# Two VectorE steps in other places: the residues of the first FFN weight pair cut in two, the sums of the second pair behind two residues of h

## The chip, the cores and the metric

One Trainium2 chip, of which the kernel uses one core. The metric is the device time of one execution in microseconds. The kernel before takes 1040.91 us, the median of 3 runs (1039.49 to 1041.45). The profile is of one further execution, which took 1038.12 us.

## The reference

One layer of a streaming encoder, in float32, for 256 rows of 2048. The input is normalised and multiplied by w_in (2048 x 5120). One part of the result goes through differential attention with 4 heads, the other through a gated causal convolution. Both results stand side by side in `mixed`, and then:

```python
h = h + jnp.einsum('bsm,md->bsd', mixed, w_out[l])
hn = rms_norm(h, norm2_g[l])
a = jnp.einsum('bsd,df->bsf', hn, w_gate[l])
bu = jnp.einsum('bsd,df->bsf', hn, w_up[l])
h = h + jnp.einsum('bsf,fd->bsd', jax.nn.silu(a) * bu, w_down[l])
```

w_out is 2048 x 2048, w_gate and w_up are 2048 x 5632, w_down is 5632 x 2048. Each weight is used once, for all 256 rows.

## The kernel before

**How a product is made.** Each float32 operand is split into a rounded part and a residue: `hi = round(a)` in a type that TensorE multiplies fast, and `lo = a - hi`. A product is then three matmuls into one PSUM bank: hi x hi, lo x hi and hi x lo. For weights, a chunk of 128 x 1024 (512 KB) is loaded by SyncE into `raw`. ScalarE casts it to `whi` (L351), and VectorE subtracts to get `wlo` (L360). For some chunks, marked `by_dma`, the residue is made without VectorE: ScalarE writes the negative rounded part (L354), and POOL issues a DMA that adds the weights to it out of memory (L355).

**Pairs and twos.** The FFN's products are run in blocks of 512 columns, each block for w_gate and w_up together (or for two column blocks of w_down). In a block, some of the rows of the weights are multiplied by a scheme of Strassen's kind with seven products instead of eight. Such a unit is a *pair* (letter s in the order of units): SyncE loads 1 MB into `wb` (four slices of 512 columns). VectorE forms the sums of slices (`pair_sums`, L1054 to L1056), three new ones in `wt` and one that replaces the first slice of `wb`. ScalarE rounds: three slices of `wb` in L1063, the replaced one in L1067, the three of `wt` in L1068, together `wh`. VectorE makes the residues `wl` in two instructions, four slices in L1072 and three in L1073. TensorE then runs seven products of three matmuls each (L1090, L1091, L1092). The remaining rows of the weights are plain units, *twos* (g for w_gate, u for w_up; a capital letter means that the residue is made by DMA): twelve matmuls each, L1114 with `whi` and L1119 with `wlo`. The first block's order is s g G u s g s G U s U u.

**The seam.** The last 512 columns of w_out are a block of eight chunks of twelve matmuls each (L390 and L391 with `whi`, L396 with `wlo`). Behind it the first FFN block begins with a pair. Around this seam:

- `make_forms` prepares the left operands of the pairs (`fhi`, `flo`) out of `hn`, the first half of the scaled rows of h, and at its end the sums, casts and residues of the first pair.
- `out_done(3)` runs when the last w_out columns stand in PSUM: VectorE adds them to h (L883), ScalarE scales the result (L894), TensorE transposes four blocks of it (L902) into a PSUM bank `ps_h`, twice. For each of the two banks ScalarE writes the rounded part (L910, two instructions), and VectorE the residue (L912, two instructions, `llo`). Later the squares of h are summed (ScalarE L528, VectorE L926), POOL turns them into the norm `rest` (L226, L227, L928), and only then does POOL issue its next residue DMA (L355).
- A bank of PSUM is reused in turn. The pair's seventh product takes the bank of the first `ps_h`, so it waits for the first two L912. A later u unit takes the bank of the second `ps_h`.

**What sets the order.** Every engine runs its list in the order in which the program emits it, waiting at each instruction for semaphores. The emission is done by `run_chunks`: before each unit `t` is multiplied, it emits the loads, sums, casts and residues of units up to some number ahead (`until(...)`), and at points inside `multiply` it calls `resume()`, which lets each running generator (`make_forms`, `out_done`, ...) go on to its next `yield`. `lag(n)` is n such yields. So a VectorE instruction's place depends on which yield emits it. `part_of(i)` emits the residues of unit i, `round_of(i)` its casts, `sums_of(i)` the sums of a pair. `raw` has four buffers in turn in the FFN, and `wb` two; a load waits until the last reader of its buffer is done, and the loads wait in one queue, SyncE's.

Of the kernel before, what the change touches and what calls it, by code (L numbers as in the profile page):

```python
# [19 lines left out]
P = 128  # L20
# [97 lines left out]
def tile_block(  # L118
# [331 lines left out]
    def sums_of(i):  # L450
        c = chunks[i]
        if "sides" in c and "t" not in c:
            load_until(i + 1, True)
            o = earlier(pair_at, i, 1)
            if o is not None:
                part_of(o)
            pair_sums(c)
# [12 lines left out]
    def round_of(i):  # L470
        if i not in rounded:
            rounded.add(i)
            load_until(i + 1, True)
            sums_of(i)
            chunks[i]["round"](chunks[i])

    def part_of(i):
        if i not in parted:
            parted.add(i)
            round_of(i)  # L480
            chunks[i]["split"](chunks[i])

    def run_chunks():
        n = len(chunks)
        pair_at.extend(i for i, c in enumerate(chunks) if "sides" in c)
        two_at.extend(i for i, c in enumerate(chunks) if "kind" in c and "sides" not in c)
        at = dict(part=0, dma=0, sums=0, round=0, minus=0, raw=0)
        first = next(i for i, c in enumerate(chunks) if "kind" in c)

        def until(what, do, stop, only=lambda c: True, may=lambda i: True):  # L490
            while at[what] < min(n, stop) and may(at[what]):
                if only(chunks[at[what]]):
                    do(at[what])
                at[what] += 1

        for t in range(n):
            if t >= first - AHEAD:
                until("part", part_of, t + 1 + (LO_AHEAD if t >= first else 1))
                until("raw", lambda i: round_raw(chunks[i]), t + 1 + RAW_AHEAD, lambda c: "sides" in c,
                      lambda i: i <= t or may_round_raw(t, i))  # L500
                ahead = SUMS_AHEAD if t >= first else 0
                until("sums", sums_of, t + 1 + ahead - ("sides" in chunks[t] and bool(chunks[t].get("prompt"))), may=may_sum)
                until("dma", round_of, t + 1 + DMA_AHEAD, lambda c: c["by_dma"])
                until("round", round_of, t + 1 + (HI_AHEAD if t > first else LO_AHEAD))
                load_until(t + 1 + LOAD_AHEAD)
            else:
                if t < len(XPARTS):
                    until("part", part_of, t + 2)
                else:
                    until("part", part_of, t + 1 + AHEAD)  # L510
                    until("minus", minus_of, min(t + 1 + MINUS_AHEAD, first), lambda c: c.get("minus"))
                    until("round", round_of, min(t + 1 + ROUND_AHEAD, first))
            part_of(t)
            chunks[t]["multiply"](chunks[t])
            if chunks[t].get("prompt") and chunks[t]["done"]:
                resume()
        while running:
            resume()
# [359 lines left out]
    def out_done(n, ps):  # L878
        cs = slice(n * N, (n + 1) * N)
        if n == D // N - 1:  # L880
            open_second()
        for m in range(NM):
            dve.tensor_tensor(h[m][:, cs], h[m][:, cs], ps[m], ALU.add)  # L883
        for m in range(NM):
            pool.dma_start(out=out[m * P : (m + 1) * P, cs], in_=h[m][:, cs])
        if n == 2:
            held[0] -= NM
        if n == 0:
            yield from open_first()
        elif n < D // N - 1:  # L890
            yield
        scaled = ffn["scaled"]
        for m in range(NM):
            act.activation(scaled[:, m], h[m][:, cs], AF.Copy, scale=rstd1[m])  # L894
        yield from lag(2)
        for t in range(0, N // P, 2):
            k = n * (N // P) + t
            yield from room(1)
            pt = aux_ps.tile([P, 2, S], F32, tag="aux", name="ps_h")
            for i in range(2):  # L900
                for m in range(NM):
                    pe.transpose(pt[:, i, m * P : (m + 1) * P], scaled[:, m, (t + i) * P : (t + i + 1) * P], ident)  # L902
            if n % 2 == 0:
                rows = ffn["hn"][:, n // 2 * NS + t : n // 2 * NS + t + 2, :]
                for i in range(2):
                    act.activation(rows[:, i, :], pt[:, i, :], AF.Copy, scale=col("g2", k + i))
            else:
                hi, lo = (a[:, t : t + 2] for a in ffn["plain"][0]) if n == 1 else lhs_two("h", k)
                for i in range(2):
                    act.activation(hi[:, i], pt[:, i], AF.Copy, scale=col("g2", k + i))  # L910
                for i in range(2):
                    dve.scalar_tensor_tensor(lo[:, i], pt[:, i], col("g2", k + i), hi[:, i].bitcast(F32),  # L912
                                             ALU.mult, ALU.subtract)
                    hT[k + i] = (hi[:, i, :], lo[:, i, :])
            yield
        if n == 2:
            start(make_forms())
        if n == D // N - 1:
            yield from lag(2)
        for m in range(NM):  # L920
            square_sum(h[m][:, cs], ss2[m][:, n : n + 1])
        if n == D // N - 1:
            yield
            for m in range(NM):
                ss = small.tile([P, 1], F32, tag="ssh", name="ssh")
                dve.tensor_reduce(ss, ss2[m], AX.X, ALU.add)  # L926
                rsqrt_mean(rest[m], ss, D, EPS)
                pool.tensor_tensor(rest[m], rest[m], rms1[:, m : m + 1], ALU.mult)  # L928
            open_third()
            yield from lag(10)  # L930
            at = slot[0] % (KD // 2) * 4 - 2 * 4
            for a, c in zip(arena, ffn["plain"][1]):
                act.copy(c, a[:, at : at + 8].rearrange("p (k m) c -> p k (m c)", m=NM))
            for k in REST:
                i, k_ = divmod(k, HK)
                plain[k] = tuple(c[:, k_ - NS] for c in ffn["plain"][i])
# [75 lines left out]
    def make_forms():  # L1012
# [25 lines left out]
        sums_of(pair_at[0])  # L1038
        round_raw(first)
        yield  # L1040
        part_of(pair_at[0])

    def load_pair(c):
# [21 lines left out]
    def round_pair(c):  # L1065
        round_raw(c)
        act.copy(c["hi"][:, 3], c["b"][:, 0])  # L1067
        act.copy(c["hi"][:, :3], c["t"])  # L1068

    def split_pair(c):  # L1070
        c["lo"] = ffn["w", c["turn"]].tile([P, 7, N], F32R, tag="wl", name="wl")
        dve.tensor_tensor(c["lo"][:, 3:], c["b"], c["hi"][:, 3:].bitcast(F32), ALU.subtract)  # L1072
        dve.tensor_tensor(c["lo"][:, :3], c["t"], c["hi"][:, :3].bitcast(F32), ALU.subtract)  # L1073

    def sum_bank(c, i):
        sums = c["sums"]
# [268 lines left out]
```

## Time and profile before

| what | before |
|---|---|
| median of the runs | 1040.91 us (1039.49 to 1041.45) |
| profiled execution | 1038.12 us |
| its span | 1036.3 us |
| TensorE busy | 1024.2 us, 99% |
| VectorE busy | 890.0 us, 86% |
| ScalarE busy | 707.9 us, 68% |
| POOL busy | 166.8 us, 16% |
| moved by DMA | 260.68 MB, 252 GB/s in the mean |

All times in the profile's rows are microseconds from the start of the span. In a timeline row the columns are start, duration, engine, line, operation, output<-inputs, shape, count, and in brackets the engine's idle time before the row with what ended it. A row of waits reads: who waited <- for whom: microseconds in total, times, the longest. A row of a window gives the window, its length, and the busy time and the number of instructions of TensorE, its weight loads, VectorE, ScalarE and POOL. Behind them stand the granted TensorE clock (1.00 is full speed), the DMA engines' busy share and GB/s. A row of DMA issues gives destination<-source, the queue, the count, KB each, and the microseconds from issue to landing. Ends of matmuls are modelled and overlap, so the distance between starts is what is counted.

### The profile page before, as it was taken

The page shows a single profiled execution, that of the slowest core. Times are in us where ns is not written, and L with a number is a line of the kernel's source. Part 1 is how long each engine was busy: PE and PEld are TensorE (multiplying, and loading weights), DVE is VectorE, ACT ScalarE, POOL GpSimd, SP SyncE. Part 2 cuts the span into 40 slices and gives each one's busy share as a digit, 9 for nine tenths or more (in the row PEclk, how much of TensorE's full clock was granted, in tenths as well). Part 3 has the DMA queues.
Part 4 walks back from the last instruction along what each step waited for, and adds up shares of the span by engine and source line. Part 5 has one row for each costly group of instructions (what it writes and reads, how often), then busy time and mean ns, then how long its engine had stood idle before and what let it go on. Part 6 is the DMA issues. An engine that isn't in the chain of part 4 may idle for free. (4 is left out here: it accounts for less than half of the span.)

```text
span 1036.3 us, 13143 instructions
## 1 busy us (share of the span) xinstructions
PE 1024.2 (99%) x4621; PEld 845.8 (82%) x4621; DVE 890.0 (86%) x1120; ACT 707.9 (68%) x940; POOL 166.8 (16%) x206
## 2 busy tenths in 40 slices
PE   9999999999999899999999999999999999999998
PEld 7888887888887688888888888888888888888887
DVE  6699889897648888999989889999898887998984
ACT  7754567857758667777665757776766576767761
POOL 0150332411100221011002020110110221101122
PEclk9999999999999999999999999999999999999999
DMA  9968665675565898798799997987979999789896
GB/s 364 311 203 247 225 204 183 193 213 183 162 228 179 291 315 241 245 311 234 251 284 253 304 265 268 312 238 247 305 236 282 271 266 329 221 266 302 236 263 131
DMA packets 65490, 260.68 MB, mean 252 GB/s; under 512 B 7312, under 2 KB 8592, under 8 KB 56976
## 3 DMA queue, kind: packets, MB, share of 16 engines
q1 hardware_dynamic: 47648, 202.13, 53.2%
q0 software_dynamic: 17344, 57.16, 29.7%
q8 instruction: 36, 0.59, 0.2%
q10 hardware_dynamic: 432, 0.55, 0.1%
q14 instruction: 30, 0.25, 0.1%
HBM read 251.42 MB, written 8.39 MB: 251 GB/s over the span
## 5 line engine op out<-in xcount | busy, mean ns | idle before, releaser
L351 ACT CAST whi<-raw 128x1024 fp32r<-128x1024 f32 (+1 forms) x246 | 253.9, 1040 | 46.3 <-PE acc L391 25.9
L360 DVE TENSOR_TENSOR wlo<-raw,whi 128x1024 fp32r<-128x1024 f32 (+1 forms) x153 | 184.0, 1208 | 45.6 <-ACT whi L351 39.8
L1063 ACT CAST wh<-wb 128x1536 fp32r<-128x1536 f32 x66 | 97.9, 1484 | 127.8 <-issue 66.3
L1072 DVE TENSOR_TENSOR wl<-wb,wh 128x2048 fp32r<-128x2048 f32 x66 | 151.0, 2287 | 37.9 <-ACT wh L1067 37.5
L355 POOL DMA_DIRECT2D wlo<-in_wts_dram x79 | 69.8, 883 | 541.9 <-ACT wlo L354 397.3
L390 PE MATMUL acc<-whi,lhi 128*128 128x512 f32 x352 | 139.0, 395 | 0.3 <-ACT whi L351 0.3
L391 PE MATMUL acc<-whi,llo 128*128 128x512 f32 x352 | 137.3, 390 | 0.0
L1090 PE MATMUL q<-wh,fhi 128*128 128x512 f32 x308 | 120.2, 390 | 2.4 <-DVE llo L912 2.4
L1092 PE MATMUL q<-wl,fhi 128*128 128x512 f32 x308 | 119.9, 389 | 0.0
L1091 PE MATMUL q<-wh,flo 128*128 128x512 f32 x308 | 119.8, 389 | 0.0
L1073 DVE TENSOR_TENSOR wl<-wt,wh 128x1536 fp32r<-128x1536 f32 x66 | 115.6, 1752 | 0.0
L604 DVE SCALAR_TENSOR_TENSOR y<-upad,cw,y 128x256 f32<-128x256 f32 x240 | 100.6, 482 | 3.4 <-ACT y L597 3.4
L1068 ACT CAST wh<-wt 128x1536 fp32r<-128x1536 f32 x66 | 97.6, 1479 | 0.0
L1119 PE MATMUL q<-wlo,chi 128*128 128x512 f32 x336 | 91.3, 393 | 0.0
L1114 PE MATMUL q<-whi,chi 128*128 128x512 f32 x336 | 89.9, 389 | 0.0
L1114 PE MATMUL q<-whi,clo 128*128 128x512 f32 x336 | 89.9, 389 | 0.0
L396 PE MATMUL acc<-wlo,lhi 128*128 128x512 f32 x304 | 83.6, 396 | 1.2 <-DVE wlo L360 1.2
L354 ACT ACTIVATE wlo<-raw 128x1024 fp32r<-128x1024 f32 x79 | 83.3, 1055 | 0.0
L1054 DVE TENSOR_TENSOR wt<-wb 128x1024 f32<-128x1024 f32 x66 | 80.5, 1220 | 0.6
L390 PEld LDWEIGHTS acc<-whi,lhi 128*128 128x128 f32 x352 | 66.1, 188 | 14.5 <-ACT whi L351 0.8
L391 PEld LDWEIGHTS acc<-whi,llo 128*128 128x128 f32 x352 | 66.1, 188 | 13.5
L1114 PEld LDWEIGHTS q<-whi,chi 128*128 128x128 f32 x336 | 63.1, 188 | 13.4
(221 smaller groups left out, 1794.2 us busy)
## 6 DMA issues: line engine op xcount, KB each, us to landing
raw<-in_wts_dram SPq DMA_DIRECT2D x242, 512.0 KB, 6.9
wb<-in_wts_dram SPq DMA_DIRECT2D x66, 1024.0 KB, 7.3
wlo<-in_wts_dram POOLq DMA_DIRECT2D x79, 512.0 KB, 9.3
lod<-in_wts_dram POOLq DMA_DIRECT2D x14, 512.0 KB, 5.9
out_dram<-sum POOLq DMA_DIRECT2D x22, 256.0 KB, 5.9
h<-in_x_dram SPq DMA_DIRECT2D x4, 512.0 KB, 9.6
out_dram<-h POOLq DMA_DIRECT2D x8, 256.0 KB, 5.8
xt<-in_xt_dram SPq DMA_DIRECT2D x6, 256.0 KB, 6.2
```

The source lines that it names most:

```text
L351: act.copy(c["hi"], c["raw"])
L360: dve.tensor_tensor(c["lo"], c["raw"], c["hi"].bitcast(F32), ALU.subtract)
L390: pe.matmul(ps[m], xhi[:, ms], hi[:, j, :], start=c["first"] and j == 0, stop=False)
L391: pe.matmul(ps[m], xlo[:, ms], hi[:, j, :], start=False, stop=False)
L604: dve.scalar_tensor_tensor(y[:, ct, :], src, wk, y[:, ct, :], ALU.mult, ALU.add)
L1063: act.copy(c["hi"][:, 4:], c["b"][:, 1:])
L1072: dve.tensor_tensor(c["lo"][:, 3:], c["b"], c["hi"][:, 3:].bitcast(F32), ALU.subtract)
L1073: dve.tensor_tensor(c["lo"][:, :3], c["t"], c["hi"][:, :3].bitcast(F32), ALU.subtract)
L1090: pe.matmul(ps, fhi[:, f, p, :], c["hi"][:, w], start=bool(first), stop=False)
L1091: pe.matmul(ps, flo[:, f, p, :], c["hi"][:, w], start=False, stop=False)
L1092: pe.matmul(ps, fhi[:, f, p, :], c["lo"][:, w], start=False, stop=bool(last))
L1114: pe.matmul(ps, plain[i][e][:, ms], hi[:, i, ns], stop=False, start=i == e == 0 and bool(c["first"].get(qs[m])))
```

## The change

Four edits in the emission. `run_chunks` looks ahead for sums only from the unit behind the first pair on. `out_done` of the last columns emits the sums of the second pair itself, right behind the residues of the first `ps_h`. The residues of a pair are emitted by `split_half`, four slices (half 0) or three (half 1), and `split_pair` emits those that are still missing. `make_forms` emits the first pair's casts, then half 0 one yield later, and half 1 two yields after that (`lag(2)`, then `part_of`).

```diff
-                ahead = SUMS_AHEAD if t >= first else 0
+                ahead = SUMS_AHEAD if t > first else 0
...
                     hT[k + i] = (hi[:, i, :], lo[:, i, :])
+                if n == D // N - 1 and t == 0:
+                    sums_of(pair_at[1])
             yield
...
         sums_of(pair_at[0])
         round_raw(first)
         yield
+        round_of(pair_at[0])
+        yield
+        split_half(first, 0)
+        yield from lag(2)
         part_of(pair_at[0])
...
+    def split_half(c, half):
+        if "lo" not in c:
+            c["lo"] = ffn["w", c["turn"]].tile([P, 7, N], F32R, tag="wl", name="wl")
+            c["split_halves"] = set()
+        if half not in c["split_halves"]:
+            c["split_halves"].add(half)
+            src, at = (c["t"], slice(0, 3)) if half else (c["b"], slice(3, 7))
+            dve.tensor_tensor(c["lo"][:, at], src, c["hi"][:, at].bitcast(F32), ALU.subtract)
+
     def split_pair(c):
-        c["lo"] = ffn["w", c["turn"]].tile([P, 7, N], F32R, tag="wl", name="wl")
-        dve.tensor_tensor(c["lo"][:, 3:], c["b"], c["hi"][:, 3:].bitcast(F32), ALU.subtract)
-        dve.tensor_tensor(c["lo"][:, :3], c["t"], c["hi"][:, :3].bitcast(F32), ALU.subtract)
+        for half in range(2):
+            split_half(c, half)
```

The lists of TensorE, ScalarE, POOL and SyncE hold the same instructions in the same order as before. VectorE's list differs at two places. Line numbers move too: what was L1054 to L1056 is L1060 to L1062 in the changed kernel, and L1072 and L1073 are both L1083.

The first place is the end of w_out. VectorE before, from the sums of the first pair (wt_3309, wb_3190) on; wlo_3324 and wlo_3340 are the residues of the seventh and the eighth of w_out's last eight chunks:

```order
L1054 TENSOR_TENSOR wt_3309<-wb_3190 128x1024
L1055 TENSOR_TENSOR wt_3309<-wb_3190,wt_3309 128x512
L1056 TENSOR_TENSOR wb_3190<-wt_3309,wb_3190 128x512
L1072 TENSOR_TENSOR wl_3321<-wb_3190,wh_3313 128x2048
L1073 TENSOR_TENSOR wl_3321<-wt_3309,wh_3313 128x1536
L360 TENSOR_TENSOR wlo_3324<-raw_3295,whi_3297 128x1024
L360 TENSOR_TENSOR wlo_3340<-raw_3307,whi_3326 128x1024
```

VectorE with the change, the same place (the two residues of w_out are now called wlo_3321 and wlo_3339, the pair's wl_3333):

```order
L1060 TENSOR_TENSOR wt_3309<-wb_3190 128x1024
L1061 TENSOR_TENSOR wt_3309<-wb_3190,wt_3309 128x512
L1062 TENSOR_TENSOR wb_3190<-wt_3309,wb_3190 128x512
L360 TENSOR_TENSOR wlo_3321<-raw_3295,whi_3297 128x1024
L1083 TENSOR_TENSOR wl_3333<-wb_3190,wh_3313 128x2048
L360 TENSOR_TENSOR wlo_3339<-raw_3307,whi_3323 128x1024
L1083 TENSOR_TENSOR wl_3333<-wt_3309,wh_3313 128x1536
```

The two residues of w_out moved forward: one ahead of both pieces of the pair's, the other between them.

The second place is some ten instructions on, behind the last sums into h. VectorE before, with the sums of the second pair (wt_3415, wb_3367) and the residues of h's last four blocks of rows (llo_97, out of the first and the second ps_h):

```order
L360 TENSOR_TENSOR wlo_3409<-raw_3354,whi_3363 128x1024
L360 TENSOR_TENSOR wlo_3413<-raw_3365,whi_3411 128x1024
L1054 TENSOR_TENSOR wt_3415<-wb_3367 128x1024
L1055 TENSOR_TENSOR wt_3415<-wb_3367,wt_3415 128x512
L1056 TENSOR_TENSOR wb_3367<-wt_3415,wb_3367 128x512
L912 SCALAR_TENSOR_TENSOR llo_97<-ps_h_3439,cols_118,lhi_96 128x256 x2
L912 SCALAR_TENSOR_TENSOR llo_97<-ps_h_3456,cols_118,lhi_96 128x256 x2
```

VectorE with the change, the same place (the first ps_h is now ps_h_3435, the sums go to wt_3444):

```order
L360 TENSOR_TENSOR wlo_3409<-raw_3354,whi_3363 128x1024
L360 TENSOR_TENSOR wlo_3413<-raw_3365,whi_3411 128x1024
L912 SCALAR_TENSOR_TENSOR llo_97<-ps_h_3435,cols_118,lhi_96 128x256 x2
L1060 TENSOR_TENSOR wt_3444<-wb_3367 128x1024
L1061 TENSOR_TENSOR wt_3444<-wb_3367,wt_3444 128x512
L1062 TENSOR_TENSOR wb_3367<-wt_3444,wb_3367 128x512
L912 SCALAR_TENSOR_TENSOR llo_97<-ps_h_3456,cols_118,lhi_96 128x256 x2
```

The first two L912 moved ahead of the three sums; the other two stay behind them.

## Prediction

> **What bounds the kernel now.** I read the page first, then TensorE's waits, then the timelines of the engines around those waits.
>
> ```profile
> span 1036.3 us, 13143 instructions
> PE 1024.2 (99%) x4621; PEld 845.8 (82%) x4621; DVE 890.0 (86%) x1120; ACT 707.9 (68%) x940; POOL 166.8 (16%) x206
> ```
>
> ```profile
> PE acc L396 <- DVE wlo L360: 3.8, 2, 2.6
> PE q L1090 <- DVE llo L912: 2.4, 1, 2.4
> ```
>
> TensorE is the bound: 1024.2 of 1036.3 us busy. What can be won is its idle time, 12.1 us with head and tail, and two waits for VectorE, 2.6 and 2.4 us, are its longest. Both lie where w_out ends and the first FFN block begins. There the PE timeline reads (start, duration, operation):
>
> ```profile
> 335.20 0.39 PE L391 MATMUL acc<-whi,mclo 128*128 128x512 f32 x1
> 338.21 1.21 PE L396 MATMUL acc<-wlo,mchi 128*128 128x512 f32 x4 [2.62 <-DVE wlo L360]
> 343.60 0.39 PE L1090 MATMUL q<-wh,fhi 128*128 128x512 f32 x1
> 346.33 0.60 PE L902 MATMUL ps_h<-ident,scaled 128*128 128x128 f32 x4
> 346.68 0.48 PE L1090 MATMUL q<-wh,fhi 128*128 128x512 f32 x1
> 348.16 0.60 PE L902 MATMUL ps_h<-ident,scaled 128*128 128x128 f32 x4
> 351.11 0.47 PE L1090 MATMUL q<-wh,fhi 128*128 128x512 f32 x1 [2.36 <-DVE llo L912]
> 351.88 1.07 PE L1114 MATMUL q<-whi,chi 128*128 128x512 f32 x4
> 352.78 1.07 PE L1114 MATMUL q<-whi,clo 128*128 128x512 f32 x4
> ```
>
> ```profile
> 336.00:338.00 2.00, 0.00 (x0) 0.00 (x0) 2.00 (x2) 2.00 (x3) 0.33 (x1) 1.00 0.00 0
> 339.30:342.80 3.50, 3.50 (x10) 2.72 (x9) 0.00 (x0) 0.00 (x0) 0.00 (x0) 0.51 0.97 215
> 348.00:351.20 3.20, 0.84 (x7) 0.55 (x6) 3.13 (x6) 2.41 (x4) 0.00 (x0) 1.00 1.01 422
> ```
>
> Four matmuls take 0.907 us at full speed (351.88 to 352.78), 0.227 each. The first wait should have ended at 335.43 and ended at 338.21: 2.78 us. The 16 matmuls from 338.21 to 343.60 should take 3.63 and take 5.39, since the granted clock falls to 0.51 for 3.5 us: 1.76 more. **The first stall costs 4.54 us**, its clock included. Four transposes take 0.35 (346.33 to 346.68), so the second wait runs from 348.51 to 351.11, 2.60 us; the clock stays at 1.00, and its first matmul starts the next 0.08 late.
>
> **The change part by part.** It moves instructions on VectorE alone; the lists of the other engines keep their order. VectorE and ScalarE there:
>
> ```profile
> 331.68 0.69 DVE L1056 TENSOR_TENSOR wb<-wt,wb 128x512 f32<-128x512 f32 x1
> 333.06 2.29 DVE L1072 TENSOR_TENSOR wl<-wb,wh 128x2048 fp32r<-128x2048 f32 x1 [0.69 <-ACT wh L1067]
> 336.94 2.35 DVE L360 TENSOR_TENSOR wlo<-raw,whi 128x1024 fp32r<-128x1024 f32 x2
> 343.34 1.28 DVE L883 TENSOR_TENSOR h<-h,acc 128x512 f32<-128x512 f32 x2 [4.05 <-PE acc L396]
> 346.37 1.23 DVE L360 TENSOR_TENSOR wlo<-raw,whi 128x1024 fp32r<-128x1024 f32 x1 [0.61 <-ACT whi L351]
> 347.51 1.22 DVE L1054 TENSOR_TENSOR wt<-wb 128x1024 f32<-128x1024 f32 x1
> 350.10 1.65 DVE L912 SCALAR_TENSOR_TENSOR llo<-ps_h,cols,lhi 128x256 fp32r<-128x256 f32 x4
> 359.38 0.21 DVE L926 TENSOR_REDUCE ssh<-ss 128x1 f32<-128x4 f32 x2
> ```
>
> ```profile
> 332.40 0.62 ACT L1067 CAST wh<-wb 128x512 fp32r<-128x512 f32 x1 [3.17 <-DVE wb L1056]
> 334.31 1.99 ACT L351 CAST whi<-raw 128x1024 fp32r<-128x1024 f32 x2
> 345.30 1.03 ACT L351 CAST whi<-raw 128x1024 fp32r<-128x1024 f32 x1
> 346.96 0.84 ACT L910 ACTIVATE lhi<-ps_h,cols 128x256 fp32r<-128x256 f32 x2 [0.63 <-PE ps_h L902]
> ```
>
> Edit one, the split in halves. The residue PE waits for (first L360 of the 336.94 row) stood behind both halves of the pair's, from 333.06. Now it follows L1056 at once: 332.4 to 333.6, before PE wants it at 335.43. The 4-slice half runs 333.5 to 335.8 (its cast ended at 333.0). The second L360 needs the cast that ends at 335.3: 335.7 to 336.9, wanted at 335.43 + 12 x 0.227 = 338.15. The 3-slice half ends near 338.6; the pair's second product reads it first, in its third matmul, at 339.06 + 5 x 0.227 = 340.20. Splitting was already two instructions, so cutting it in two places adds none, and all of it lies beside 28 matmuls that have their operands. The slack of each step is 1.2 us or more; a cast that comes later than that costs PE the excess one for one. Behind the 3-slice half stands L883, which PE's last w_out matmuls release at 338.8: nothing is held up. All 4.54 us should go: PE starts the pair at 343.60 - 4.54 = 339.06. Were the residue merely exchanged for another wait at the pair's second product, the gain of this edit would fall towards nothing; the 1.6 us between 338.6 and 340.20 speak against it.
>
> Loads: the first moved L360 frees the buffer that SyncE's next load of raw waits for, so this load and the megabyte for pair 2 queued behind it start about 4.6 us sooner, at 333.6 and 334.0, while the DMA engines carry 0 GB/s (row 336 to 338). Such a megabyte takes 7.3 us in the median:
>
> ```profile
> wb<-in_wts_dram SPq DMA_DIRECT2D x66, 1024.0 KB, 7.3
> ```
>
> It lands near 341.3.
>
> Edit two, the sums of pair 2 (L1054 to L1056) between the two pairs of L912. PE wants the bank at 348.51 - 4.54 = 343.97. L910 moves with the transposes to 342.42, ends at 343.26, and two L912 take about 0.88, to 344.17. L1090 follows 0.1 later: 344.28. A wait of 0.31 stays, plus the 0.08, so PE ends this product (351.11 to 351.88, 0.77) at 345.05 instead of 351.88: **6.83 us earlier**. The sums themselves begin at 344.1, with their megabyte there, and the second pair of L912, now behind them, ends near 347.6; the bank that it frees is wanted two units of 12 matmuls on, at 345.05 + 2 x 2.72 = 350.5. So the reordering costs nothing there, up to 2.9 us.
>
> VectorE is free for the first L912 at 343.1: L883 after PE's last matmul, 338.8 to 340.1, one L360 to 341.2, the next after its cast (341.9) to 343.1. This needs its raw landed by 340.86; that load took 5.3 us:
>
> ```profile
> raw<-in_wts_dram SPq DMA_DIRECT2D x1, 512.0 KB, 5.3
> ```
>
> Issued near 333.6, it lands near 338.9, 2 us early. If this cover is gone, the cast, L360 and L912 follow one for one, and the old wait is back at 2 us of lateness.
>
> What is late next. VectorE does not gain 6.8: from L912 to L926 it took 359.38 - 350.10 = 9.28 us, and now the sums (350.10 - 347.51 = 2.59) lie between too: L926 at 343.29 + 11.87 = 355.16, **4.22 earlier**. Behind L926, POOL computes rest and then issues the DMA that makes the residue of a U unit:
>
> ```profile
> 359.62 2.22 POOL L226 TENSOR_SCALAR rsq<-ssh 128x1 f32<-128x1 f32 x1 [1.18 <-DVE ssh L926]
> 364.86 0.64 POOL L226 TENSOR_SCALAR rsq<-ssh 128x1 f32<-128x1 f32 x1
> 367.33 0.93 POOL L355 DMA_DIRECT2D wlo<-in_wts_dram  x1 [0.47 <-issue]
> ```
>
> ```profile
> 376.81 1.07 PE L1119 MATMUL q<-wlo,chi 128*128 128x512 f32 x4
> ```
>
> ```profile
> wlo<-in_wts_dram POOLq DMA_DIRECT2D x1, 512.0 KB, 7.7
> ```
>
> ```profile
> DMA to landing us min/median/max: 7.7/8.5/11.2
> ```
>
> ```profile
> DMA to landing us min/median/max: 5.5/9.3/13.9
> ```
>
> (The last two: this kind of DMA from 300 to 400 us, and in the whole span.) It landed at 375.0, 1.8 us before use. Now: issue 363.11; landing after 7.7 is 370.8, after the 8.5 of its neighbours 371.6; PE wants it at 369.98. So a **new wait of 0.8 to 1.6 us**, which no wait of the old profile shows. I take 1.2; the bounds are none (landing in 5.5 or 6.8) and 7.0 (13.9). POOL's queue holds nothing for PE but later residues, the next with 4 us to spare.
>
> The sum rests on POOL's chain staying 367.33 - 359.62 = 7.71 us long. Its first round takes 5.24 (359.62 to 364.86), its second, of the same three instructions, 2.0 (to 367.33 less the 0.47 of issue). The long ones lie beside VectorE's L1072 and L1073, which stand behind L926 in the new list as in the old, so I keep 7.71. Were the first round as short as the second, the residue would land 3.2 sooner, at 367.6, and the wait would be none: this is most of rival A.
>
> [...]
>
> Sum: 6.83 - 1.2 = 5.6 us. Profiled execution 1038.12 (span 1036.3 and 1.8 around it) to 1032.5. The median of the runs, 1040.91, stands 2.8 above that execution; I take the gain from it: **1035.3**. After that PE's lead should last, since the helpers wait for PE, not the reverse:
>
> ```profile
> ACT wh L1063 <- PE q L1091: 59.5, 22, 5.2
> ```
>
> **Rivals.** (A) No new wait: POOL's chain shortens, or the DMA lands within 6.8 us. For it: 5.5 occurs in the span; against: 7.7 is the least of this stretch. The gain is 6.83: 1034.1.
>
> (B) The second stall mostly stays, since L912 still stands behind an L360 whose raw lands late. It decides from 340.86 on. The next load of raw, issued at 339.1 into a crowd of others, took
>
> ```profile
> raw<-in_wts_dram SPq DMA_DIRECT2D x1, 512.0 KB, 9.3
> ```
>
> With that the raw is there at 342.9, the L360 done at 345.1, L912 at 346.0, and L1090 starts 1.9 later; VectorE and PE slip together, so the new wait stays: 6.83 - 1.9 - 1.2 = 3.7, 1037.2. Against it: the DMA engines are idle when this load is issued.
>
> (C) The lead is not kept, because the loads set the pace of the FFN blocks:
>
> ```profile
> DMA  9968665675565898798799997987979999789896
> ```
>
> Many slices behind the 13th show 9 tenths. If PE only meets the same landings sooner, most of 5.6 us returns as waits on casts and residues: 1039 to 1041. Against it: PE waits for nothing of the kind in the old profile, and ScalarE waits 59.5 us for PE's buffers. VectorE as the pace alone would not do it, being itself 4.2 us earlier (1036.7).
>
> (D) Slower: the new wait itself. If the U residue lands over 12.0 us after its issue, at 375.1 or later, PE idles 5.1 us, the clock halves for 1.76 more, and the 6.83 is gone. At 13.9 it is 7.0 + 1.8 = 8.8 against 6.8, 2.0 slower: 1042.9. For it: two such DMAs are issued back to back here, and more loads come early. Against: 11.2 is the most in this stretch.
>
> That the change does not do what it says is excluded: the order shows it.
>
> [...]
>
> **How the numbers follow.** Forecast 0.52, its own range 1034.0 to 1036.6 (a wait of 0.8 to 1.6, and about 1 us for the runs' spread); A 0.20; B 0.12; C 0.10; D 0.06. 0.2% is 2.1 us, about what a measurement tells from no change, so forecast, A and B are faster (0.84), C is the same (0.10), D slower (0.06). The range reaches from 1033.0, A less 1.1, to 1038.8, where B's slip has nearly doubled and C begins; C, D and the tails stay outside, about 0.2.
>
> **What would show it.** Right: no L396 wait behind 335 us, no 0.5 clock near 340, L1090's wait on L912 under 0.5, a wait of L1119 on a wlo DMA near 370, all later work about 5.6 earlier. Wrong: L360 or L912 still among TensorE's waits of over 1 us, a wait on a landing of several us, or waits of PE on casts and residues after 400 us.

## The result, and the profile after

The changed kernel takes 1032.26 us (median of 1031.05 to 1032.47) against 1040.22 for the kernel before (1039.49 to 1041.45) on the same chip: a ratio of 0.992, 95% interval 0.9903 to 0.9937. Two later sets on one chip gave 1031.41 against 1039.15 (0.9919, 0.9906 to 0.9933) and 1031.61 against 1039.04 (0.9935, 0.9921 to 0.9948). So the change gains 7.4 to 8.0 us. The forecast was 5.6 us and 1035.3: the right direction, but too little by some two microseconds, and the measured time lies 0.7 us below the predicted range. The ratios and their 95% intervals are estimates of their own, not quotients of the two medians; they differ from those by up to 0.0008, which is 0.8 us, so gains of this size are not known to a tenth. One run of the kernel before, of 1473.14 us at a mean clock of 0.655, stands apart from all others and is left out everywhere.

The profiled execution took 1031.05 us. Its page begins:

```profile
span 1029.3 us, 13143 instructions
PE 1022.3 (99%) x4621; PEld 844.9 (82%) x4621; DVE 890.3 (86%) x1120; ACT 708.0 (69%) x940; POOL 164.2 (16%) x206
```

The span is 7.0 us shorter with the same number of instructions, and TensorE's busy time fell by only 1.9, about the 1.76 of the half clock; the rest was idle time. TensorE's largest waits behind the start of the kernel:

```profile
PE acc L390 <- ACT whi L351: 0.6, 2, 0.4
PE acc L396 <- DVE wlo L360: 0.5, 1, 0.5
```

Both waits of over 2 us are gone, and no wait for a landing has come in. The wait of 0.5 for L360 lies far ahead of the change, at 162.5 us, where the input is multiplied by w_in. It stood there before, too: the old row was 3.8 us in two waits, 1.2 of it near 162 us and 2.6 at the end of w_out. TensorE's timeline around the two places and at the use of the U residue:

```profile
335.13 1.07 PE L396 MATMUL acc<-wlo,mchi 128*128 128x512 f32 x4
...
337.85 1.07 PE L396 MATMUL acc<-wlo,mchi 128*128 128x512 f32 x4
338.76 0.39 PE L1104 MATMUL q<-wh,fhi 128*128 128x512 f32 x1
...
343.31 0.60 PE L902 MATMUL ps_h<-ident,scaled 128*128 128x128 f32 x4
344.01 0.47 PE L1104 MATMUL q<-wh,fhi 128*128 128x512 f32 x1
...
344.79 1.08 PE L1128 MATMUL q<-whi,chi 128*128 128x512 f32 x4
...
369.75 1.08 PE L1133 MATMUL q<-wlo,chi 128*128 128x512 f32 x4
```

The first row stands where the old kernel stalled for 2.62 us: it follows without a gap. From it to the pair's first product 3.63 us pass (338.76 - 335.13), 16 matmuls at 0.227, where 5.39 passed before. Behind the transposes at 343.31 (0.35 for four) the product starts at 344.01, so 0.35 us is left of the wait that was 2.60. The product behind it ends at 344.79 instead of 351.88. Part of that is a lead of 0.30 that this execution already had ahead of the change (the last L391 starts at 334.90, against 335.20); 6.79 us is the change's. The granted clock there:

```profile
336.00:338.00 2.00, 2.00 (x10) 1.65 (x10) 2.00 (x2) 1.91 (x3) 0.62 (x1) 1.00 1.06 446
338.00:340.00 2.00, 2.00 (x11) 1.65 (x10) 1.71 (x4) 0.78 (x2) 0.68 (x2) 1.00 1.00 410
```

Full speed, where the old profile had 0.51, and the DMA engines are busy throughout (1.06, 446 GB/s) where they had carried nothing: the next loads do start sooner. VectorE at both places:

```profile
331.38 0.69 DVE L1062 TENSOR_TENSOR wb<-wt,wb 128x512 f32<-128x512 f32 x1
331.98 1.22 DVE L360 TENSOR_TENSOR wlo<-raw,whi 128x1024 fp32r<-128x1024 f32 x1
333.12 2.29 DVE L1083 TENSOR_TENSOR wl<-wb,wh 128x2048 fp32r<-128x2048 f32 x1
335.32 1.22 DVE L360 TENSOR_TENSOR wlo<-raw,whi 128x1024 fp32r<-128x1024 f32 x1
336.46 1.75 DVE L1083 TENSOR_TENSOR wl<-wt,wh 128x1536 fp32r<-128x1536 f32 x1
338.50 1.28 DVE L883 TENSOR_TENSOR h<-h,acc 128x512 f32<-128x512 f32 x2 [0.29 <-PE acc L396]
...
342.99 0.88 DVE L912 SCALAR_TENSOR_TENSOR llo<-ps_h,cols,lhi 128x256 fp32r<-128x256 f32 x2 [0.23 <-ACT lhi L910]
343.78 1.22 DVE L1060 TENSOR_TENSOR wt<-wb 128x1024 f32<-128x1024 f32 x1
...
354.87 0.21 DVE L928 TENSOR_REDUCE ssh<-ss 128x1 f32<-128x4 f32 x2
```

The first L360 ends at 333.2, 1.9 us before TensorE wants it, the second at 336.5, 1.3 before. L912 now waits for ScalarE's L910, not behind the sums. POOL's chain and its DMA for the U residue:

```profile
355.11 2.22 POOL L226 TENSOR_SCALAR rsq<-ssh 128x1 f32<-128x1 f32 x1 [1.06 <-DVE ssh L928]
...
360.34 0.64 POOL L226 TENSOR_SCALAR rsq<-ssh 128x1 f32<-128x1 f32 x1
...
362.82 1.83 POOL L355 DMA_DIRECT2D wlo<-in_wts_dram  x2 [0.47 <-ACT wh L1073]
```

```profile
wlo<-in_wts_dram POOLq DMA_DIRECT2D x1, 512.0 KB, 6.7
```

From 355.11 to 362.82 is 7.71 us, what the chain took before. Landing 6.7 us after its issue the residue is there at 369.5, and TensorE uses it at 369.75 without a wait.

### The profile page after: what moved, and what is told of

Same layout as the page of the kernel before. It is cut to its first block, busy times and chain, and to the rows that moved or that the text cites. A ratio compares the mean times of both kernels' runs of the same rounds, so it can differ in the third digit from the quotient of the medians.

```text
span 1029.3 us, 13143 instructions
## 1 busy us (share of the span) xinstructions
PE 1022.3 (99%) x4621; PEld 844.9 (82%) x4621; DVE 890.3 (86%) x1120; ACT 708.0 (69%) x940; POOL 164.2 (16%) x206
## 5 line engine op out<-in xcount | busy, mean ns | idle before, releaser
L360 DVE TENSOR_TENSOR wlo<-raw,whi 128x1024 fp32r<-128x1024 f32 (+1 forms) x153 | 183.9, 1207 | 42.2 <-ACT whi L351 40.4
L1083 DVE TENSOR_TENSOR wl<-wb,wh 128x2048 fp32r<-128x2048 f32 x66 | 150.9, 2287 | 36.8 <-ACT wh L1073 36.5
L391 PE MATMUL acc<-whi,llo 128*128 128x512 f32 x352 | 137.3, 390 | 0.0
L1083 DVE TENSOR_TENSOR wl<-wt,wh 128x1536 fp32r<-128x1536 f32 x66 | 115.6, 1751 | 0.0
L1133 PE MATMUL q<-wlo,chi 128*128 128x512 f32 x336 | 91.3, 394 | 0.0
L1060 DVE TENSOR_TENSOR wt<-wb 128x1024 f32<-128x1024 f32 x66 | 80.5, 1220 | 0.6
L391 PEld LDWEIGHTS acc<-whi,llo 128*128 128x128 f32 x352 | 66.1, 188 | 13.5
```

Source lines behind the costliest of these rows:

```text
L360: dve.tensor_tensor(c["lo"], c["raw"], c["hi"].bitcast(F32), ALU.subtract)
L391: pe.matmul(ps[m], xlo[:, ms], hi[:, j, :], start=False, stop=False)
L1083: dve.tensor_tensor(c["lo"][:, at], src, c["hi"][:, at].bitcast(F32), ALU.subtract)
L1133: pe.matmul(sum_bank(c, qs[m])[:, ns], plain[i][0][:, ms], lo[:, i, ns], start=False, stop=i == 1 and ns.stop == N and bool(c["last"].get( ...
```

## The experiments

Each edit is given against the changed kernel. Gains are differences of medians from the kernel before within the same set. In the sets behind the result, 49 runs of the kernel before, beside which the other kernels ran, have a median of 1039.15 us, and nine of the changed kernel 1031.57.

### The two kernels again

The kernel before, unchanged:

> The kernel before, unchanged, once more: what do its executions differ in? In the profile of before the second stall left the clock at full speed, in the profiled execution, which took 1038.1 us; the timed runs took 1039.5 to 1041.5. Theory (clock lottery): a stall of 2.6 us sometimes ends in a second stretch of halved clock of 3.4 us, 1.7 us longer; then the mean granted clock of its runs falls in steps (0.998 for one stretch of 3.4 us in 1036, 0.997 for two), and the long runs are those with the lower clock. Rival (plain spread): runs with the same mean clock differ by as much as the others. Ratio to before: 1.000 in both.

1039.03 us (1037.55 to 1040.59), ratio 0.9998 (0.9989 to 1.0007) to its twin. The 1040.91 shown ahead of the forecast was the median of three runs; the median of 49 is 1.8 lower. Its profile, in stretches around both stalls:

```profile
338.00:339.30 1.30, 1.30 (x4) 1.01 (x4) 0.78 (x1) 0.00 (x0) 0.06 (x1) 0.50 0.48 79
...
351.20:352.00 0.80, 0.80 (x3) 0.61 (x3) 0.80 (x1) 0.80 (x2) 0.00 (x0) 0.50 1.02 420
```

Here the second stall halved the clock too (0.50 from 351.2), which in the first profile stayed at 1.00. The half clock comes in stretches of 3.41 us: the traces of this case record five in the middle of the program, four of 3.413 us and one of twice that. One such stretch lowers the mean clock of a 1036 us span by 0.0016, and the runs' mean clocks fall in two groups: 0.998 in 21 of the 49 (median 1038.57), 0.997 in 28 (median 1039.30). By that reading every run of the kernel before pays for at least one half-clock stretch, and more than half of them for two. What the second stretch costs can be read off the two profiles: from the pair's first product to the first L1119, 10.09 us pass in the first (343.60 to 353.69), where the second stall left the clock up, and 11.77 in this one (342.81 to 354.58), 1.68 more, of which 0.09 is a longer wait. The two groups of runs lie less far apart, 0.73 us in the medians and 0.98 in the means; why they do is not shown.

The changed kernel, unchanged, twice:

> The changed kernel once more. Clock lottery: no stall, so a mean clock of 1.000 in every run, and a spread of the spans well under 1.7 us. Rival (plain spread): a spread like that of before. Both: about 8 us faster than before by the medians, about 7 by the spans of executions of before with one stretch of halved clock.

> The changed kernel once more, beside the next three. If the new wait for the U unit's residue exists in some executions and not in others (its DMA took 6.7 us in one profile of this kernel and 7.5 in another, with 0.0 and 0.56 us of wait), its runs spread over about 1 us at a clock of 1.000 or 0.999; else all spans lie within 0.3 us of 1029.3.

1031.41 and 1031.61 us, with clocks of 0.999 to 1.000 in every run. The runs of the second set spread over 1.1 us. The wait for the U residue came in both profiles, 0.56 and 0.41 us. First the one, then the other:

```profile
370.57 1.16 PE L1133 MATMUL q<-wlo,chi 128*128 128x512 f32 x4 [0.56 <-DMA wlo<-in_wts_dram]
```

```profile
370.04 1.16 PE L1133 MATMUL q<-wlo,chi 128*128 128x512 f32 x4 [0.41 <-DMA wlo<-in_wts_dram]
```

Counted by starts, as the prediction counts, these matmuls come 0.72 and 0.58 us late (370.57 against 368.94 + 0.91, 370.04 against 368.55 + 0.91). So the new wait exists in two executions of three, but costs 0, 0.72 and 0.58 us, not 0.8 to 1.6.

### Each edit alone

Edit one alone, the residues in two pieces, with the sums looked for where they were before:

```diff
-                ahead = SUMS_AHEAD if t > first else 0
+                ahead = SUMS_AHEAD if t >= first else 0
...
-                if n == D // N - 1 and t == 0:
-                    sums_of(pair_at[1])
```

> Only the first edit: the residues of the first pair in two pieces, the sums of the second pair ahead of all four residues of h as before. By the prediction's steps the first stall and its halved clock go (4.54 us) and the second stall stays at 2.6 us: span 4.5 us below that of before, with one wait of TensorE on L912 of 2.4 to 2.6 us. Clock lottery: runs in two groups 1.7 us apart, mean clock 1.000 and 0.998. Plain spread: no such groups. Rival on the first edit: the stall moves to the pair's second product, and the gain is under 2 us.

1034.60 us, ratio 0.9948 (0.9936 to 0.9961): a gain of 4.55, against 4.54 worked out. That they agree to a hundredth is luck, since the interval of the ratio reaches from 4.1 to 6.7 us. Of the two stalls only the second is left:

```profile
347.10 0.47 PE L1102 MATMUL q<-wh,fhi 128*128 128x512 f32 x1 [2.38 <-DVE llo L912]
```

Its five runs fall in two groups:

```
mean clock 1.000: 1033.49 1034.09
mean clock 0.998: 1034.60 1035.04 1035.19
```

The same stall of 2.4 us halves the clock in three runs of five. The means of the two groups lie 1.15 us apart, where 1.7 was expected. In the profiled execution the clock stayed up, and there the stall is what the prediction took it for: from the second set of transposes to the product behind the stall 3.74 us pass (344.13 to 347.87), with the whole change 1.48 (343.31 to 344.79), so it costs 2.26; the prediction has 2.29 (6.83 - 4.54).

Edit two alone, the sums behind the first residues of h, with the first pair's residues made at once as before:

```diff
-        round_of(pair_at[0])
-        yield
-        split_half(first, 0)
-        yield from lag(2)
         part_of(pair_at[0])
```

> Only the second edit: the sums of the second pair between the residues of h, the residues of the first pair in one go ahead of the two of w_out as before. By the prediction's steps the first stall stays (2.6 us of wait and 1.76 of halved clock), and the second shrinks from 2.60 to about 0.3: span 2.3 us below before. Rival: L912 now stands behind an L360 whose raw lands late in this order (343.5), so the second stall hardly shrinks, gain under 1 us. Clock lottery: every run has one stretch of halved clock, 0.998.

1035.76 us, ratio 0.996 (0.9947 to 0.9972): a gain of 3.39, where 2.3 was expected. Four of the five runs have a clock of 0.998 and one 1.000. The second stall is gone from the profile, and the first is there with its half clock:

```profile
337.70 2.08 PE L396 MATMUL acc<-wlo,mchi 128*128 128x512 f32 x4 [2.62 <-DVE wlo L360]
```

```profile
337.20:338.60 1.40, 0.90 (x2) 0.80 (x3) 1.40 (x2) 0.48 (x1) 0.85 (x1) 0.50 0.00 0
```

The two gains add up to 7.94, the whole change gives 7.74 in this set: there is no sign that the edits touch each other. On top of edit one, edit two gives 3.19 (1034.60 - 1031.41); the forecast had 2.29 for it, less the new wait. This is where the gain was undersized. By the spread of these nine runs, the 3.19 is known to about 0.9 either way (an estimate).

### What a stall costs, by its length

To price a stall by itself, the residue that stands ahead of the first L912 (the L360 before it) is computed two, three and four times, which changes nothing in the result and sets back VectorE there and POOL's chain behind it:

```diff
-            dve.tensor_tensor(c["lo"], c["raw"], c["hi"].bitcast(F32), ALU.subtract)
+            for _ in range(1 + (1 if c is chunks[pair_at[0] + 3] else 0)):   # then 2, then 3
+                dve.tensor_tensor(c["lo"], c["raw"], c["hi"].bitcast(F32), ALU.subtract)
```

> The changed kernel with the residue ahead of the residues of h computed twice: 1.14 us of VectorE work ahead of L912, a wait of TensorE of about 1.2 us near 343.7. Lottery by a free-running window of 3.4 us: a wait this short never empties enough of a window, all runs at 0.999 to 1.000, 0.9 us slower than the changed kernel. Rival (any stall of about 1 us can halve the clock): some runs at 0.998, 1.2 to 1.7 us longer.

> The changed kernel with the residue ahead of the residues of h computed three times: 2.28 us of VectorE work ahead of L912, so that a second stall of the old length is back (TensorE waits 2.3 to 2.5 us near 343.7) with the order of the change. Clock lottery: the stall alone costs 2.0 us against the changed kernel; in some of the runs a stretch of 3.4 us at half clock comes on top, 1.2 to 1.7 us, and those runs show a mean clock lower by 0.001 to 0.002. Rival (the clock is not drawn by chance, only by the length of the stall): all runs alike, 2.0 us slower at a clock of 1.000, since 2.4 us left it at full speed in the profile of before.

> The changed kernel with that residue computed four times: 3.42 us of VectorE work, a wait of about 3.4 us. Lottery by a free-running window of 3.4 us: the longer the wait, the more of its places in the window halve the clock; nearly all runs at 0.998, 3.1 us of wait and 1.2 to 1.7 us of clock, 4.3 to 4.8 us slower than the changed kernel. Rival (the share of runs with a halved clock doesn't depend on the length): about half of the runs, as with the stall of 2.3 us.

Waits at this place, in the profile of each in turn:

```profile
PE q L1105 <- DVE llo L913: 1.0, 1, 1.0
```

```profile
PE q L1105 <- DVE llo L913: 2.3, 1, 2.3
```

```profile
PE q L1105 <- DVE llo L913: 3.6, 1, 3.6
```

| wait there, us | median, us | above the changed kernel, 1031.6 | runs at a clock of 0.998 or less |
|---|---|---|---|
| 1.0 | 1032.62 | 1.0 | 0 of 5 |
| 2.3 | 1034.21 | 2.6 | 2 of 5 |
| 3.6 | 1036.54 | 4.9 | 11 of 11, 5 of them at 0.997 or 0.996 |

The first and the third ran on another chip than the changed kernel; the kernel before takes the same there (1039.18 against 1039.04 and 1039.15). In the profiles of the first two the U residue is late again, by a wait of 0.7 and 0.5 us, so the table prices a stall together with what it delays. The ratios to the kernel before are 0.9935 (0.9922 to 0.9949), 0.996 (0.9947 to 0.9972) and 0.9977 (0.9968 to 0.9986). In the profiled execution of the 2.3 us wait, the clock stays at full speed:

```profile
347.00:352.00 5.00, 5.00 (x23) 4.11 (x23) 4.93 (x7) 3.48 (x5) 0.00 (x0) 1.00 0.52 210
```

In that of the 3.6 us wait it is 0.54 for six microseconds, two stretches:

```profile
345.00:348.00 3.00, 0.31 (x1) 0.34 (x2) 2.97 (x5) 1.36 (x2) 0.00 (x0) 0.79 1.03 318
348.00:354.00 6.00, 6.00 (x16) 4.67 (x16) 5.93 (x7) 3.81 (x6) 0.00 (x0) 0.54 0.35 141
```

So the half clock follows a stall with a chance that grows with its length: none at 1.0 us, about half at 2.3 and 2.4, four of five at 2.6, all at 3.6. The runs at 2.3 us whose clock stayed up lie 2.1 to 2.6 us above the changed kernel, the two others 3.8 and 4.3. Either case alone misprices the stall. The counts of five are small, so the chances are rough.

Where the chance comes from can be read off the traces. All changes of clock that a trace records lie whole multiples of 3.413 us apart, so the clock goes by a fixed grid of such windows, and TensorE's busy time in each can be looked up. The 16 traces of this case hold 4798 whole windows at full clock. Behind each of the 17 in which TensorE was busy for 1.36 us or less, the clock was halved (5 at stalls, 12 at the program's end); behind each of the 4781 in which it was busy for 1.58 us or more, it was not. The two windows at this border, of edit two alone and of edit one alone:

```profile
333.72:337.14 3.42, 1.36 (x7) 0.78 (x5) 3.42 (x3) 3.42 (x5) 0.00 (x0) 1.00 0.00 0
```

```profile
345.27:348.68 3.41, 1.58 (x7) 1.36 (x8) 3.38 (x7) 3.41 (x4) 0.00 (x0) 1.00 1.02 308
```

| stall | wait, us | window of the grid | TensorE busy in it, us | clock of the next window |
|---|---|---|---|---|
| before, first profile, first stall | 2.62 | 335.94 to 339.35 | 1.14 | 0.50 |
| before, first profile, second stall | 2.36 | 349.59 to 353.01 | 1.90 | 1.00 |
| before again, first stall | 2.62 | 333.79 to 337.21 | 1.29 | 0.50 |
| before again, second stall | 2.44 | 347.45 to 350.86 | 0.97 | 0.50 |
| edit two alone, first stall | 2.62 | 333.72 to 337.14 | 1.36 | 0.50 |
| edit one alone, second stall | 2.38 | 345.27 to 348.68 | 1.58 | 1.00 |
| added stall of 1.0 | 1.04 | 342.97 to 346.38 | 2.37 | 1.00 |
| added stall of 2.3 | 2.30 | 344.64 to 348.06 | 2.01 | 1.00 |
| added stall of 3.6 | 3.57 | 343.30 to 346.71 | 0.82 | 0.50 |

What decides is therefore how much of a stall falls into one window. If a stall begins anywhere on the grid with equal chance and needs 1.9 us of idle time in one window (between 3.41 - 1.58 and 3.41 - 1.36), it halves the clock in 0.5 to 0.6 of the executions at 2.3 to 2.6 us, in 0.9 at 3.6 and never at 1.0: an estimate, and near the counts.

### The cut of the first pair's residues

With the early half left out, both residues of w_out stand ahead of the whole pair's:

```diff
-        split_half(first, 0)
         yield from lag(2)
```

> The residues of the first pair in one go, but behind both residues of w_out (the cut undone, the move kept). Theory (the cut buys the time of both sides): the four-slice part starts 1.2 us later than with the cut, the three-slice part ends near 340.6, so TensorE waits about 0.5 us at the pair's second product, the sums into h (released at 338.5) start near 340.6, 2.1 us late, and with them the scaling, the transposes and the residues of h: the seventh product about 1.6 us later than in the changed kernel, all in all 1.3 to 2 us slower than it. Rival (the cut is of no use, only the order matters): within 0.3 us of the changed kernel.

1033.30 us, ratio 0.9937 (0.9924 to 0.995): 1.7 to 1.9 over the changed kernel, as much as expected. Its waits:

```profile
PE q L1132 <- DMA wlo<-in_wts_dram: 0.8, 1, 0.8
PE q L1103 <- DVE llo L912: 0.5, 1, 0.5
PE q L1105 <- DVE wl L1082: 0.2, 1, 0.2
```

The pair's residue now comes 0.2 late, and with it all that VectorE does behind it. The largest of the waits, for the U residue, is not among the parts that the expectation added up, so the amount is right in part by luck. With the two-yield lag left out as well, the whole of the pair's residues lies between the two of w_out:

```diff
-        split_half(first, 0)
-        yield from lag(2)
```

> The residues of the first pair in one go between the two residues of w_out. Theory: the second residue of w_out ends at 338.3, TensorE wants it near 337.85, a wait of about 0.5 us on L360; what follows shifts by the same: 0.4 to 0.6 us slower than the changed kernel. Rival: the cut is worth more than 1 us or nothing.

1032.74 us, ratio 0.9935 (0.9923 to 0.9947), and a wait of 0.3 for the second residue:

```profile
PE acc L396 <- DVE wlo L360: 0.3, 1, 0.3
```

That is 1.1 to 1.3 over the changed kernel's medians, more than the 0.4 to 0.6 expected, but the runs (1031.08 to 1034.27) and the interval cover the changed kernel's own: what the cut into two pieces gives over this order is not settled. Most of edit one's gain lies in where the residues of w_out stand.

### The new wait: the U residue's landing

Four kernels move the DMA that makes the U residue. First, the sums stand behind all four L912, so that VectorE's own chain comes later:

```diff
-                if n == D // N - 1 and t == 0:
+                if n == D // N - 1 and t == 2:
```

> The sums of the second pair behind all four residues of h instead of between them. Theory (the U residue is next): the second two residues of h wait for their casts until 344.8, the sums, the casts of pair 2 and all VectorE work behind come 1.5 us later, POOL's chain and the U unit's residue with them; that landed 0.25 us before its use in the changed kernel, so TensorE now waits 1.2 to 1.4 us for this DMA near 369.5, and the kernel is 1.2 to 1.4 us slower than the changed one. Rival (VectorE has slack there): the same within 0.3 us.

```profile
371.39 1.16 PE L1133 MATMUL q<-wlo,chi 128*128 128x512 f32 x4 [1.35 <-DMA wlo<-in_wts_dram]
```

The wait came as expected, 1.35 us. The median, 1034.76 (0.995, 0.9936 to 0.9963), is 3.2 over the changed kernel, more than the wait: its six runs spread from 1031.49 to 1035.63, and the three longest (from 1035.00 on) are those with clocks of 0.998 and 0.997. Which stall halves the clock in them was not seen, since the profiled execution is one of the others (1032.81); a run at full clock took 1034.52, for which no cause was seen either.

Then the residue of the first two chunks behind the second pair, which stands ahead of the sums that feed POOL's chain, is computed two and three times, by the edit of the stall kernels with another index:

```diff
+            for _ in range(1 + (1 if c is chunks[pair_at[0] + 5] else 0)):   # then 2
```

> The changed kernel with one residue of 1.14 us (that of the first two behind pair 2) computed twice on VectorE, right ahead of the sums of squares that POOL's chain waits for. Theory (the U residue is next, margin 0.25 us): POOL issues that DMA 1.14 us later, TensorE waits 0.8 to 0.9 us for it, 0.8 to 0.9 us slower than the changed kernel. Rival (the DMA lands as early as it is needed, or the margin is larger): no wait, the same within 0.2 us.

> The changed kernel with the residue of the first two behind pair 2 computed three times, 2.28 us of VectorE work ahead of POOL's norm chain. Theory (the U residue is next; it lands 5.2 to 7.7 us after issue): issue near 365.1, landing 370.3 to 372.8, use at 369.75: a wait of 0.6 to 3.1 us on this DMA in every execution, 1.5 to 2.2 us slower than the changed kernel in the median. Rival (the DMA is as early as its use demands): within 0.5 us of the changed kernel.

The first: 1031.83 us (0.9933, 0.9919 to 0.9947), and no wait in the profiled execution, against the expectation. The DMA was issued at 364.08, 1.26 later than in the first profile of the changed kernel, and landed sooner after its issue:

```profile
wlo<-in_wts_dram POOLq DMA_DIRECT2D x1, 512.0 KB, 5.2
```

But the profiled execution (1031.08) is one of three short runs; the three others took 1032.57, 1032.75 and 1035.10, the last at a mean clock of 0.997. What they waited for was not seen. A stall long enough to halve the clock came in one of them, so a wait for this residue, and a long one, is not excluded.

The second: issued at 365.65, 2.83 later, and a wait of 1.16, yet only 0.6 us in the median (1032.21; 0.9939, 0.9926 to 0.9951), where 1.5 to 2.2 was expected:

```profile
371.34 1.17 PE L1134 MATMUL q<-wlo,chi 128*128 128x512 f32 x4 [1.16 <-DMA wlo<-in_wts_dram]
```

Last, that DMA ahead of POOL's norm chain, by holding the sums that feed the chain back for three yields:

```diff
         if n == D // N - 1:
-            yield
+            yield from lag(3)
             for m in range(NM):
```

> The changed kernel with POOL's norm chain (rest) behind the U unit's residue DMA instead of ahead of it, and the sums of squares behind the residues of the third pair. Theory (this wait is what is left): the DMA is issued near 358 instead of 362.8 and lands near 365, 4 us ahead of use, no wait in any execution; spans near 1029 with less spread, 0.2 to 0.6 us faster than the changed kernel in the median. Rival (the spread has another source): the same median and spread as the changed kernel. Second rival: the residue behind it, of the second U unit, now stands behind POOL's chain, is issued near 367.4 and is late: up to 1 us slower.

POOL issues the DMA 4.4 us sooner, TensorE uses the residue without a wait, and the second U unit's residue (the second rival) doesn't make it wait either; POOL's row, then TensorE's:

```profile
358.44 0.89 POOL L355 DMA_DIRECT2D wlo<-in_wts_dram  x1 [4.28 <-ACT wlo L354]
```

```profile
369.83 1.07 PE L1133 MATMUL q<-wlo,chi 128*128 128x512 f32 x4
```

1031.56 us (0.9932, 0.9919 to 0.9944), against 1031.61 for the changed kernel in the same set. The 0.2 to 0.6 us hoped for is not there, and its runs spread as widely (1030.94 to 1033.20). So what is left of the new wait is worth no more than this spread hides, some tenths of a microsecond. No kernel tried beats the changed one. The spread between runs at full clock lies in good part ahead of the change: the last L391 ahead of the seam starts between 334.46 and 335.72 us in the 16 profiled executions, though the edits move nothing ahead of 330 us. The wait for L360 near 162 us, 1.23 in the first profile of before and 0.48 in the first of the changed kernel, is one source; the others were not sought.

## Why the prediction was right or wrong

**The first stall: right.** 4.54 us were worked out; alone it measured 4.55, with luck in the last digits. In the profile the residue follows L1062, nothing halves the clock, the pair starts 4.84 earlier (343.60 to 338.76), of which 0.30 is the lead that the execution had ahead of it, and no other wait took the place. The loads start sooner, as forecast.

**The second stall: order and wait right, price wrong.** 0.31 us was to be left of it and 0.35 is; 6.83 earlier was forecast for the product behind it, and 6.79 was seen. The failing step is "the clock stays at 1.00", which was taken from one execution. In more than half the runs of the kernel before (28 of 49, by their mean clock of 0.997) the clock has two half-clock stretches, and in the profile that shows them the second lies at this stall. At full clock the stall costs 2.26, as worked out. A second stretch, 1.68 dearer in that profile, in 28 of 49 runs adds 0.96 to it (an estimate; 0.4 to 0.6 by the distance of the two groups of runs), and put on top of edit one, edit two gives 3.19, so **this term was about 0.9 too small**.

**VectorE and POOL: right.** L926, now L928, was to come 4.22 earlier and came 4.51 earlier, 4.21 without the lead of 0.30. POOL's chain was to stay 7.71 long and did. L226 again took 2.22 us in the first round, beside VectorE's L1083 of 2.28 us, which ends at 357.28 where L226 ends at 357.33, and 0.64 in the next round, beside the shorter L1061 of 0.69. That the first round is long because of the VectorE instructions beside it was the author's estimate from such rows; no run tried it by itself.

**The new wait: place right, size wrong.** The failing step is "I take 1.2". Issue (363.11 forecast, 362.82 seen) and use (369.98, 369.75) were right; the landing was not. It was priced at 7.7 to 8.5 us from the old execution's row and its neighbours, and took 6.7, 7.5 and 7.3 in the changed kernel's three profiles. By starts the wait was 0, 0.72 and 0.58, 0.43 in the mean, and taking it away moves nothing that can be measured: **about 0.8 too much taken off**. The first profile met the bound "none"; rival A, for which 6.83 was given, was the nearest.

The two steps together account for the gain: 5.6 + 0.9 + 0.8 = 7.3, against 7.74 and 7.43 measured in the later sets and 7.96 in the first. The difference is within what these medians leave open; the sizes of the two steps were taken from the runs afterwards, so the sum is no test of its own.

**The anchor.** The profiled execution before took 1038.12, the 49 runs have a median of 1039.15, and the 1040.91 that the gain was taken from lies 1.8 above that. The forecast kept all 2.8 us between that median and the profiled execution for the changed kernel, too. About 1 us of the distance was the second stall's half clock, which the change removes, and the rest the chance of three runs. From 1039.15 the forecast gain gives 1033.5, within the predicted range.

**The rivals.** B, the second stall staying for a late load, fell: L912 waits for L910. C, the lead given back to the loads, fell: the span is 7.0 shorter. D, a landing over 12 us, was not seen: the longest landing of this residue in a profile was 9.0, in the kernel that issues it first, and no run of the changed kernel has a mean clock under 0.999. Of the cues, the first and the second showed, and the shift of all later work, by 6.8 us (beside the lead of 0.3) instead of 5.6; the wait on L912 is under 0.5; the wait of L1119 (now L1133) came in two profiles of three.

## What to carry to other kernels

Price a stall of 2 to 3 us as its length plus a chance of half clock behind it (here up to 1.7 us in about half to four fifths of the runs), whatever the one profiled execution shows; the mean clock of each run tells how often it came (one stretch lowers it by 0.0016 here). Here a stall with up to 1.83 us of idle time in any one window (TensorE busy for 1.58 or more) never halved the clock. When a gain is taken from a median, ask first whether what lies between that median and the profiled execution is the very thing that the change removes. A wait that hangs on one transfer's landing is better entered with the spread of such landings (here 5.2 to 9.0 us), and with its lower bound where the work behind it has slack, than with the last landing seen.

## What the runs showed of the hardware

**The half clock comes by the place of a stall on a grid of 3.41 us.** A stall of 2.3 to 2.6 us halved it in some runs and not in others of the same kernel (2 of 5 at 2.3, 3 of 5 at 2.4, 4 of 5 at 2.6); 1.0 us never did (0 of 5), and 3.6 us always (11 of 11), in the profiled one for two stretches on end. The changes of clock of a trace lie whole multiples of 3.413 us apart. In the traces here, 2.05 us of idle time in one window sufficed for half clock (TensorE busy for 1.36) and 1.83 did not (busy for 1.58), without an exception in 4798 windows. A halved clock stayed halved behind the one window with TensorE busy for 2.43 us, and was full again behind the five with 2.85 or more. Busy times go by modelled ends of matmuls, so these borders are rough.

**The same transfer lands 5.2 to 9.0 us after its issue.** The U residue's 512 KB took 9.0 us to land when issued at 358.44, 6.7 from 362.82, 5.2 from 364.08 and 5.6 from 365.65, though also 7.5 from 362.94, and 7.7 from 364.06 in the kernel with the cut undone. Issuing it 2.83 us later moved its use by 1.6 us (369.75 to 371.34), 0.3 of it a lag that this execution had ahead of the change. Its time was not to be read off one execution's row; what makes it differ was not tried.
